# Attention's projection as two groups of seven block products, and the gate work that moves into the attention

## Chip, cores and metric

One core of a Trainium2 chip runs the kernel. The metric is the device time of one execution in microseconds, as the median of several runs; a profiled execution adds a trace of every engine: TensorE (PE, with its weight loads PEld), VectorE (DVE), ScalarE (ACT), GpSimd (POOL) and the queue engine SyncE (SP).

## What is computed

One layer of a transformer block over 512 tokens of width 2048, in fp32, with 256 context tokens. Cut to what matters here:

```
h   = rmsnorm(x) * (1 + scale) + shift                 # shift, scale, gate = silu(c) @ w_ada + b_ada
q, k, v, z_a, u_b, z_b, g_a, g_b = split(h @ w_in)     # 12 query heads, 4 key/value heads of 128
y_a = (attention(q, k, v) * silu(z_a)) @ w_proj_a      # 512 x 1536 times 1536 x 2048
y_b = (fourier_mix(u_b) * silu(z_b)) @ w_proj_b        # 512 x 512  times  512 x 2048
y   = (sigmoid(g_a) * y_a + sigmoid(g_b) * y_b) @ w_out
out = rmsnorm(x + gate * y) * final_g
```

## The kernel before

**Products.** Every fp32 operand is split into two fp32r parts, `hi` on ACT (line 163) and `lo = value - hi` on DVE (line 164), and a product is three matmuls (`mm3`, lines 311 to 313): hi x hi, hi x lo, lo x hi. A matmul is 128 x 128 against 128 x 512. Weights come in pieces of 128 x 1024 (512 KB); SP asks for them into a few raw slots (tiles `wr`), and each is split before PE uses it.

**Groups of seven block products.** The projections of `w_in` and `w_out` are done by a scheme of the Strassen kind (class `Group`, lines 756 to 852): rows, inner dimension and columns are halved, and seven products of blocks take the place of eight. `PRODUCTS` (line 55) names them P1, Q5, P2, Q6, P7, Q3, Q4. Some use sums of weight blocks. These are built in a chain: a tile `R` per piece (`chain`) holds the first block, is split for P1, then a DMA that adds (`accum_op`, issued by POOL, line 267) puts the next block on it, it is split for Q5, and so on for Q6 and Q4. `OUT_GROUP` (line 58) is the order P1, P2, Q5, Q6, P7, Q3, Q4. Results in PSUM are copied or subtracted out by ACT and DVE after a product.

**Attention** (lines 1135 to 1278). A loop of 48 steps (12 heads x 4 blocks of 128 queries): scores on PE, the maximum on DVE (line 1180), the exponential on ACT (line 1182), transposes on PE (line 1198), a split on ACT and DVE, and every second step the product with the values. What comes out is multiplied with the gate `z` (lines 1221 and 1222), kept per head in `branch`, and split into `S`. Between these steps PE gets 64 portions of the Fourier branch's projection (`filler`, line 1136): one bank of PSUM at a time, copied by ACT into `ybs` (line 1156).

**Attention's projection** (`products`, line 1229, and the loop at 1336). Four chunks of 512 columns in the order 0, 2, 1, 3. Each goes through six weight pieces (pairs of heads) with 24 matmuls a piece, over four banks of PSUM: 576 matmuls. The first chunk's first pieces run in the last steps of the attention. In this loop DVE also does three other things. It multiplies the Fourier chunks with their gate `gb` (line 1353). It works on the modulation's gate: 32 pieces `w_gate` of 128 x 1024 are multiplied with the condition row `crow` and summed along the row (`use_gate`, line 1038). And it multiplies each finished chunk with its gate `ga` and adds the Fourier part (lines 1372 and 1373). The merged chunk is transposed on PE (line 1299), and the sums and splits of token blocks that the output projection needs (`form`, line 1307) follow as `jobs`, one to a weight piece.

**Output projection.** Two groups of seven, 8 and 9, of four pieces a product.

**What sets the order.** Each engine works in order. A scheduler lays out the order within each engine at build time from the program's order and its own estimates; `issue_after` and `manual_schedule` pin some places. Slots for tiles are handed out by `take` and `give`, and a new user of a slot waits for the old one's last access. DMA queues are SP's (weights), ACT's (stores of projections) and POOL's (heads, gates, adding DMAs).

## Time and profile before

| what | us |
|---|---|
| median of 3 runs (1321.52 to 1322.96) | 1321.84 |
| span of the profiled execution, first to last instruction | 1320.2 |
| start to 822: all projections of `w_in`, the Fourier mix | 822 |
| attention, 822 to 1020 | 198 |
| attention's projection, 1020 to about 1155 | 135 |
| output projection and end, to 1320.2 | 165 |

The profiled execution's own time is taken as its span; the runs' median lies 1.6 us above it. The profile lists, for each engine, how long it was busy, what it waited for and who released it; a stretch of the span can be asked for by itself. Start times are microseconds from the span's first instruction.

### The profile page before, as it was taken

How to read it: one execution, taken by the hardware profiler on the slowest of the kernel's cores; microseconds unless marked ns; L12 is line 12 of the kernel's file. 1: busy time of each engine (PE TensorE's matmuls, PEld its weight loads, DVE VectorE, ACT ScalarE, POOL GpSimd, SP SyncE). 2: the span in 40 equal slices, each digit the busy share in tenths (PEclk: the TensorE clock that was granted, in tenths of full speed). 3: DMA queues.
4: the chain of work that ended last, by engine and by line, in shares of the span. 5: the costliest groups of instructions: out<-in, count | busy, mean ns of one | idle time of the engine just before them, and what ended most of it. 6: DMA issues, size and time to landing. Idle time of an engine off the chain costs nothing.

```text
span 1320.2 us, 17480 instructions
## 1 busy us (share of the span) xinstructions
PE 1296.7 (98%) x6594; PEld 1061.2 (80%) x6594; DVE 975.0 (74%) x1289; ACT 653.3 (49%) x1020; POOL 144.0 (11%) x192
## 2 busy tenths in 40 slices
PE   6999999999999999999999999999999999999997
PEld 3577887888888888888888887888888888888885
DVE  5666899878788868646487666677776789777676
ACT  5222655555555554444354454666666133355544
POOL 0110011110201111011031110000000100111210
PEclk9999999999999999999999999999999999999999
DMA  9898587887898998877669886122013889678985
GB/s 383 339 374 327 182 237 200 227 229 219 205 319 195 295 271 248 284 165 191 192 170 317 221 241 215 48 72 81 33 65 112 319 331 331 189 173 222 225 206 173
DMA packets 96228, 291.26 MB, mean 221 GB/s; under 512 B 8976, under 2 KB 32272, under 8 KB 91792
## 3 DMA queue, kind: packets, MB, share of 16 engines
q1 hardware_dynamic: 48720, 163.65, 35.4%
q0 software_dynamic: 22800, 96.49, 30.4%
q10 hardware_dynamic: 24624, 30.02, 6.6%
q8 instruction: 51, 0.84, 0.3%
q14 instruction: 33, 0.27, 0.1%
HBM read 263.37 MB, written 26.75 MB: 220 GB/s over the span
## 4 chain that ended last, share of the span: by engine, by line
PE 93%; DVE 3%; DMA 2%; issue 1%; ACT 1%; SPq 0%; DVEq 0%; ACTq 0%
PE banks L311 11%; PE banks L312 11%; PE banks L313 11%; PE x L312 8%; PE x L313 8%; PE x L311 8%; PE y L312 7%; PE y L313 7%; PE y L311 7%; PE banks L1198 3%; PE pd L493 2%; PE pb L311 2%; PE pb L313 1%; PE pb L312 1%; DMA wa<-in_w_ss 1%; PE pc L311 1%
## 5 line engine op out<-in xcount | busy, mean ns | idle before, releaser
L163 ACT ACTIVATE whi<-wr 128x1024 fp32r<-128x1024 f32 (+1 forms) x129 | 135.2, 1051 | 161.8 <-PE banks L313 91.5
L164 DVE TENSOR_TENSOR wlo<-wr,whi 128x1024 fp32r<-128x1024 f32 (+1 forms) x129 | 156.2, 1214 | 54.7 <-ACT whi L163 54.4
L164 DVE TENSOR_TENSOR wlo<-R,whi 128x1024 fp32r<-128x1024 f32 x114 | 138.8, 1222 | 68.5 <-ACT whi L163 68.5
L163 ACT ACTIVATE whi<-R 128x1024 fp32r<-128x1024 f32 x114 | 120.5, 1059 | 136.6 <-PE x L313 41.2
L311 PE MATMUL banks<-whi,s 128*128 128x512 f32 x420 | 165.9, 395 | 1.7 <-DVE ev L798 1.5
L312 PE MATMUL banks<-wlo,s 128*128 128x512 f32 x420 | 164.8, 392 | 0.0
L313 PE MATMUL banks<-whi,s 128*128 128x512 f32 x420 | 164.3, 391 | 0.0
L311 PE MATMUL x<-whi,s 128*128 128x512 f32 x352 | 137.3, 390 | 0.0
L313 PE MATMUL x<-whi,s 128*128 128x512 f32 x352 | 137.1, 389 | 0.0
L312 PE MATMUL x<-wlo,s 128*128 128x512 f32 x352 | 137.1, 389 | 0.0
L311 PE MATMUL y<-whi,s 128*128 128x512 f32 x316 | 123.2, 390 | 0.0
L312 PE MATMUL y<-wlo,s 128*128 128x512 f32 x316 | 123.0, 389 | 0.0
L313 PE MATMUL y<-whi,s 128*128 128x512 f32 x316 | 122.9, 389 | 0.0
L267 POOL DMA_DIRECT2D R<-in_w_g x64 | 55.4, 866 | 418.7 <-DVE wlo L164 234.6
L311 PEld LDWEIGHTS banks<-whi,s 128*128 128x128 f32 x420 | 78.9, 188 | 18.0 <-ACT whi L163 1.9
L163 ACT ACTIVATE s<-wr 128x512 fp32r<-128x512 f32 (+2 forms) x93 | 61.4, 678 | 63.4 <-PE y L312 16.3
L313 PEld LDWEIGHTS banks<-whi,s 128*128 128x128 f32 x420 | 78.9, 188 | 16.4
L312 PEld LDWEIGHTS banks<-wlo,s 128*128 128x128 f32 x420 | 79.0, 188 | 14.8
L164 DVE TENSOR_TENSOR s<-wr,s 128x512 fp32r<-128x512 f32 (+2 forms) x93 | 67.3, 751 | 21.4 <-ACT s L163 20.4
L313 PEld LDWEIGHTS x<-whi,s 128*128 128x128 f32 x352 | 66.1, 188 | 13.7
L311 PEld LDWEIGHTS x<-whi,s 128*128 128x128 f32 x352 | 66.1, 188 | 13.7
L312 PEld LDWEIGHTS x<-wlo,s 128*128 128x128 f32 x352 | 66.1, 188 | 13.6
(283 smaller groups left out, 2770.5 us busy)
## 6 DMA issues: line engine op xcount, KB each, us to landing
wr<-in_w_g SPq DMA_DIRECT2D x128, 512.0 KB, 4.9
R<-in_w_g POOLq DMA_DIRECT2D x64, 512.0 KB, 6.4
wa<-in_w_ss POOLq DMA_DIRECT2D x26, 1024.0 KB, 8.1
R<-in_w_g SPq DMA_DIRECT2D x32, 512.0 KB, 5.2
wr<-in_w_pab SPq DMA_DIRECT2D x32, 512.0 KB, 5.1
wr<-in_w_gate SPq DMA_DIRECT2D x32, 512.0 KB, 5.5
wr<-in_w_o SPq DMA_DIRECT2D x24, 512.0 KB, 6.6
R<-in_w_o POOLq DMA_DIRECT2D x24, 512.0 KB, 8.1
```

Of the source, the lines that this page charges most:

```text
L163: first = nc.scalar.activation(hi, src, ACT.Copy)
L164: return first, nc.vector.tensor_tensor(lo, src, hi.bitcast(F32), op=ALU.subtract)
L267: nc.gpsimd.dma_start(chain[e.pc], e.nxt, accum_op=ALU.add)
L311: nc.tensor.matmul(o, ah, bh, start=start, stop=False, skip_group_check=cont)
L312: nc.tensor.matmul(o, ah, bl, start=False, stop=False, skip_group_check=cont)
L313: nc.tensor.matmul(o, al, bh, start=False, stop=stop, skip_group_check=cont)
L493: last = nc.tensor.matmul(acc[32 * j : 32 * j + 32, :256], c2[:, 8 * h + k, :], w[:, k, :], start=n < 4, stop=n >= KK - 4)
L1198: nc.tensor.transpose(tp[:, k * P : (k + 1) * P], p[:, k * P : (k + 1) * P], ident)
```

## The change

Attention's result no longer goes through plain products. Its 1536 inner dimension is halved (heads 0 to 5 and 6 to 11), the tokens are halved (256 each) and the columns are two chunks each in two groups: group 10 has chunks 0 and 2, group 11 chunks 1 and 3. Each group is seven block products in `OUT_GROUP`'s order with three pieces a product. P7's weights are a raw block onto which a POOL DMA adds a second one (`onto`); Q4's are a fourth link of the chain. P1 of group 10 stands where the first chunk's first pieces stood, in the last steps of the attention.

```diff
-BRANCH_A, BRANCH_B = (0, 1, 2, 3, 4, 5), (6, 7)
+BRANCH_A, BRANCH_B = 10, (6, 7)
+A_CHUNKS = ((0, 2), (1, 3))
...
             e.raws.append((p, raw))
+            if e.onto is not None:
+                nc.gpsimd.dma_start(raw, e.onto, accum_op=ALU.add)
...
-    def stream_product(name, g, w, by_dve):
+    def stream_product(name, g, w, by_dve, pieces=4):
...
-            if isinstance(what, tuple):
+            if isinstance(what, tuple) and name == "P7" and g >= BRANCH_A:
+                stream(key, [part(1)], 1024, 2, pc=pc, onto=part(2))
+            elif isinstance(what, tuple):
...
-                       nxt=part(what + 1) if what < 2 and what + 1 not in by_dve else None)
+                       nxt=part(what + 1) if what < (3 if g >= BRANCH_A else 2) and what + 1 not in by_dve else None)
...
-    for n, j in enumerate(CHUNKS):
-        for pc in BRANCH_A:
-            stream(("pab", j, pc), w_pab[j, pc], 1024, 2)
+    for n in range(2):
+        for name in OUT_GROUP:
+            stream_product(name, BRANCH_A + n, BranchWeights(n), (), 3)
```

The Fourier branch gets its gate inside the attention: DVE multiplies each portion out of PSUM with the gate, which POOL's DMA has loaded into one of the chain's tiles or a slot, in place of ACT's copy, and the result goes to memory (`yb_d`).

```diff
-                nc.scalar.copy(y[:, t % 2, :], acc)
+                nc.vector.tensor_tensor(y[:, t % 2, :], acc, y[:, t % 2, :], op=ALU.mult)
+                if t % 2:
+                    nc.gpsimd.dma_start(yb_d[t // 2, j], flat(y))
```

Attention's output is kept per pair of heads (`AT`), its token halves are split as blocks A11, A12 and A22, and four forms of sums and differences are made for each of three pairs of pairs, two of them in the loop and one at its end.

```diff
+    def branch_forms(q):
+        u, v = AT[q], AT[q + 3]
+        lo, hi = slice(0, 256), slice(256, 512)
+        branch_form("S3", q, u[:, :, lo])
+        nc.vector.tensor_tensor(u[:, :, hi], u[:, :, hi], v[:, :, hi], op=ALU.subtract)
+        branch_form("Z5", q, u[:, :, hi])
...
```

The modulation's gate leaves DVE and the old projection loop. In steps 2 to 38 of the attention POOL multiplies the two halves of each row of weights with the condition row and adds them, 48 units in all, and ACT sums along the row. Both condition rows are now loaded and put through silu at the start of the attention. The 32 loads of `w_gate` move with them.

```diff
+    def gate_unit(u):
+        kb, part = divmod(u, 3)
+        if part < 2:
+            w = gw[part] = get_aside(("gate", kb + KK * part))
+            if kb + 1 < KK:
+                ask_gate(kb + 1 + KK * part)
+            nc.gpsimd.tensor_tensor(w, w, crow[part], op=ALU.mult)
+        else:
+            w = gw[0]
+            nc.gpsimd.tensor_tensor(w, w, gw[1], op=ALU.add)
+            nc.scalar.activation(w, w, ACT.Copy, scale=0.5, accum_out=gparts[:, kb : kb + 1])
...
+        if i >= 2:
+            for u in range(4 * (i - 2) // 3, min(4 * (i - 1) // 3, 3 * KK)):
+                gate_unit(u)
```

A finished chunk half is multiplied with its gate, a POOL DMA adds the Fourier part from `yb_d` to it, and five pieces later in the program it is transposed. The forms for the output projection are tied to counts of pieces (`after`, `form_at`).

```diff
+    def branch_done(n, half, c, v, t):
+        j = A_CHUNKS[n][c]
+        t = take((2, 512)) if t is None else t
+        w = ga.pop((half, j))
+        nc.vector.tensor_tensor(t, v, w, op=ALU.mult)
+        give(w)
+        nc.gpsimd.dma_start(flat(t), yb_d[half, j], accum_op=ALU.add)
+        merged[j, half] = t
+        after(5, lambda: turn_merged(j, half))
```

Smaller edits: weights of `V` are split only when they are due; the heads' loads come one step later; the old loop with `products`, `use_gate` and its gate loads is gone.

More of the change, by code (lines that the diff above doesn't have):

```diff
@@ L726, in pair @@
     def pair(tag, skip=0):
+        if isinstance(tag, int):
+            return banks[0][:, tag : tag + 2, :] if tag < 6 else banks[1]
         if banks:
@@ L769, in run, with steps @@
         def run(self, name):
+            for _ in self.steps(name):
+                pass
+        def steps(self, name):
             form, which = next((f, c) for n, f, _, c in PRODUCTS if n == name)
```

281 lines of the change are left out of this document (160 added, 121 removed).

## Prediction

> **What bounds the kernel now.** First the page's head, then the chain that ended last, then the windows of the stages that the change touches. The columns of a window row: its length, busy us and count of PE, PEld, DVE, ACT, POOL, then the granted clock, the DMA share and GB/s.
>
> ```profile
> span 1320.2 us, 17480 instructions
> PE 1296.7 (98%) x6594; PEld 1061.2 (80%) x6594; DVE 975.0 (74%) x1289; ACT 653.3 (49%) x1020; POOL 144.0 (11%) x192
> ...
> PE 93%; DVE 3%; DMA 2%; issue 1%; ACT 1%; SPq 0%; DVEq 0%; ACTq 0%
> ```
> ```profile
> 822.00:1020.00 198.00, 196.65 (x1305) 171.74 (x1303) 145.42 (x251) 125.12 (x221) 4.58 (x9) 1.00 0.21 71
> 1020.00:1060.00 40.00, 40.00 (x189) 33.52 (x187) 28.96 (x35) 9.25 (x10) 5.96 (x12) 1.00 0.83 305
> 1060.00:1100.00 40.00, 40.00 (x191) 33.38 (x190) 35.50 (x45) 12.22 (x15) 1.06 (x2) 1.00 0.90 334
> 1100.00:1150.00 50.00, 50.00 (x234) 41.69 (x233) 40.91 (x49) 19.31 (x23) 3.68 (x5) 1.00 0.80 261
> 1150.00:1235.00 85.00, 84.77 (x379) 69.63 (x379) 64.00 (x55) 43.90 (x52) 15.01 (x18) 1.00 0.82 196
> ```
>
> TensorE bounds every stage: it never stops in the projection (1020 to 1150) and stands still for 1.35 of 198 us in the attention, at full clock. So a matmul taken out is worth its whole cadence, and a stall put in costs its whole length: there is no slack on PE to pay for it. Beside it the attention uses the DMA engines at 0.21 and POOL for 4.6 us, and the projection uses the DMA engines at 0.80 to 0.90.
>
> **What it removes.** The old projection is 4 chunks x 6 weight pieces x 24 matmuls = 576 of 128x512. The new one is 2 groups x 7 products x 3 pieces x 12 = 504; transposes (64), score, value and Fourier matmuls stay. So 72 go. Their cadence stands in the timeline of the old projection:
>
> ```profile
> 1039.93 0.39 PE L313 MATMUL banks<-whi,s 128*128 128x512 f32 x1
> ...
> 1045.82 0.39 PE L312 MATMUL banks<-wlo,s 128*128 128x512 f32 x1
> ```
>
> Between these two starts lie 26 matmuls: 5.89 / 26 = 0.2265 us each. 72 x 0.2265 = **16.3 us less**, if nothing new stalls PE.
>
> **What it moves into the attention: the gate sums.** 32 products on DVE (1.22 us each, hidden in the old projection) become 32 products and 16 sums on POOL, with 16 passes on ACT that add up along the row. Operations of this kind POOL does nowhere in the old trace, so I bound one:
>
> ```profile
> L443 POOL MEMSET s<- 128x512 f32 x1 | 0.5, 529 | 0.0
> L1627 POOL MEMSET const-bfloat16-1.0<- 128x1 bf16 x1 | 0.1, 106 | 0.0
> L871 POOL TENSOR_SCALAR small<-small 128x8 f32<-128x8 f32 (+2 forms) x11 | 5.9, 534 | 100.7 <-ACT cxe L968 63.4 <-DVE small L986 18.4 <-ACT y L883 17.7
> L1050 POOL DMA_DIRECT2D s<-qz_d x12 | 6.4, 534 | 169.8 <-PE banks L313 47.4 <-DVE s L164 37.5 <-issue 28.0
> ```
>
> A fill costs (529 - 106) / 511 = 0.83 ns per element, one stream. 1024 elements at one stream: 0.11 + 0.85 = **0.95 us**, the low end. Arithmetic on 8 elements costs 0.53; with two reads and a write one after another, 0.53 + 3 x 0.85 = **3.1 us**, the high end. I take 0.53 + 2 x 0.85 = **2.2 us**, nearest to the arithmetic row, with the two reads in turn and the write beside them. A page gives a price: by the Trainium skill, "GPSIMD Engine Reference", section 3 "Performance versus the Vector engine", an fp32 tensor_tensor of 2048 elements takes 4497 ns on GpSimd, so about 2.3 us for 1024 (an estimate from that page), by which the sum below would be some 2 us higher; no run here shows it yet.
>
> 48 x 2.2 = 106 us of POOL would hide in 198. But the engines run in order, and in the built order ACT's passes stand between the exponentials: pass 1 ahead of exponential 1, pass 2 ahead of exponential 2, 3 ahead of 4, 4 ahead of 5, 5 ahead of 7, 6 ahead of 8, 8 ahead of 12, 10 ahead of 17. Behind a pass wait the exponential, then its transposes on PE, and PE has nothing else in its order. And the gate's weight loads wait for slots that the gate before gives back: SP loads one part of pair k+1 when POOL's sum k is done, the other when a pass is done. The rows for this ladder, by the old clock:
>
> ```profile
> 807.89 1.23 DVE L798 TENSOR_TENSOR ev<-y,ev 128x1024 f32<-128x1024 f32 x1 [2.26 <-PE y L313]
> ...
> L1031 DVE SCALAR_TENSOR_TENSOR s<-s,s 128x1024 f32<-128x1024 f32 x1 | 1.2, 1224 | 0.0
> ```
> ```profile
> L1030 ACT ACTIVATE s<-s 128x1024 f32<-128x1024 f32 x1 | 1.1, 1053 | 0.0
> L1182 ACT ACTIVATION_READ_ACCUMULATOR s<-banks,gain 128x1 f32 x48 | 9.4, 196 | 0.0
> wr<-in_w_gate SPq DMA_DIRECT2D x1, 512.0 KB, 3.7
> ```
> ```profile
> 814.51 1.06 ACT L163 ACTIVATE whi<-wr 128x1024 fp32r<-128x1024 f32 x1 [1.23 <-PE x L313]
> 825.09 0.90 ACT L1182 ACTIVATE s<-banks,gain 128x768 f32<-128x768 f32 x1 [1.06 <-DVE gain L1180]
> 827.51 0.90 ACT L1182 ACTIVATE s<-banks,gain 128x768 f32<-128x768 f32 x1 [0.95 <-DVE gain L1180]
> 865.46 0.90 ACT L1182 ACTIVATE s<-banks,gain 128x768 f32<-128x768 f32 x1 [0.39 <-DVE gain L1180]
> ```
>
> The condition row is ready behind that eviction and one 1.22 us product: 807.89 + 1.23 + 1.22 = 810.3. Sum 1: three POOL operations and one DMA issue, 810.3 + 6.6 + 0.53 = 817.4; its pass (1.05 + 0.20 = 1.25) ends at 818.7. Sum 2: a load (3.7 and 0.3 for its issue = 4.0), four POOL operations (one belongs to pair 3) and an issue: 818.7 + 4.0 + 8.8 + 0.53 = 832.0. Exponential 2 stands behind its pass: 833.3 in place of 827.5, 5.8 late. Sums 3 to 5 have one part loaded early: 4.0 + 2 x 2.2 = 8.4 each, 857.2. Sums 6 to 8 wait for both parts: 4.0 + 3 x 2.2 = 10.6 each, 889.0. Pass 8 and a weight split (1.06) then stand ahead of exponential 12: 891.3 in place of 865.5, **26 us late**. Pass 10 is no later, and after exponential 17 no pass stands until exponential 24, so POOL gets ahead. PE cannot make up lost time: the attention grows by 26 us. With 0.95 us the same ladder gives, behind the split that ends at 815.6, 816.8 for pass 1 and 825.1 for sum 2, which then waits for exponential 1; steps of 5.9, then of 7.4 (the pass and a load now limit); exponential 12 is 2 to 4 late: **3**. With 3.1 us: 838.3, steps of 10.2 and 13.3, 908.8: **46**.
>
> **The rest of what moves there.** DVE gets 16 products in place of ACT's 16 copies, 8 splits and 8 sums of the forms and a few more: some 36 operations of 0.69 us, 25 us on top of 145.4 of 198; ACT loses 16 copies (0.585) and gets 16 passes and 8 splits, 17 us more on 125.1. Both fit beside PE; if that cover fails, it fails by the order above, already counted. I cost them at nothing.
>
> **The branch groups.** Weights now go through a chain in SBUF to which a DMA adds the next block. Prices from the old output projection, where such adds run (its 75 us from 1160 to 1235; the row "to landing" is that of the chain's transfers between 1150 and 1260):
>
> ```profile
> DMA packets 4166, 15.22 MB, mean 203 GB/s; under 512 B 460, under 2 KB 460, under 8 KB 4162
> ## 3 DMA queue, kind: packets, MB, share of 16 engines
> q0 software_dynamic: 2002, 7.30, 54.0%
> q1 hardware_dynamic: 2160, 7.87, 30.3%
> ```
> ```profile
> DMA to landing us min/median/max: 3.9/7.6/16.3
> 1240.00:1250.00 10.00, 10.00 (x46) 8.20 (x45) 5.58 (x5) 5.96 (x8) 4.53 (x6) 1.00 1.05 213
> L1198 PE MATMUL banks<-ident,s 128*128 128x128 f32 x288 | 43.3, 277 | 0.1
> ```
>
> q0 carries the adds: 0.540 x 75 / 7.30 = 5.55 us per MB, 2.9 us for one of 0.524 MB. A plain load: 0.303 x 75 / 7.87 = 2.89 us per MB, 1.5 us. From the attention's end to the last product of group 2 the built order has about 26 adds (17 on the chain, 4 on a raw tile, 5 or 6 of the merged chunks) and 34 plain transfers, the first loads of the output projection among them: 26 x 2.9 + 34 x 1.5 = 126 us. PE needs 468 x 0.2265 + 48 transposes x 0.15 = 113 us. If the DMA engines work at the 1.05 that a 10 us window reached, 126 / 1.05 = 120 us: **8 us of stall** (rounded up from 7, for the third block product, due 8.2 us after the second with a median add of 7.6, and the first turned chunk, due 8.2 us after a 1.2 us product and that add). Bounds: 0 (attention's free DMA takes more of it early; the old output projection ran at 0.82 with 0.23 us of PE idle) and 18 (126 - 113 and two late adds).
>
> **Sum**, against the profiled execution's own 1320.2: -16.3 + 26 + 8 = +17.7, 1337.9. The median of the runs shown, 1321.84, lies 1.6 above that span: **1339.5 us**.
>
> **Rivals.** *A, faster:* POOL's operation near a fill's 0.95 us. For it: 0.83 ns per element; against it: 0.53 us for 8 elements of arithmetic. -16.3 + 3 + 8 = -5: 1316.5, and 1308 without the DMA stall. It decides at the price where the ladder costs 8.3: (8.3 - 3) / (26 - 3) of the way from 0.95 to 2.2, 1.24 us. *B, dearer POOL:* 3.1 us, because POOL and DVE hold each other up at SBUF. -16.3 + 46 + 8: 1359. Against it: in the attention DVE's operations with both inputs in SBUF are few:
>
> ```profile
> L164 DVE TENSOR_TENSOR wlo<-wr,whi 128x1024 fp32r<-128x1024 f32 x9 | 11.0, 1224 | 1.8 <-ACT whi L163 1.8
> L164 DVE TENSOR_TENSOR s<-s,s 128x512 fp32r<-128x512 f32 x11 | 7.5, 686 | 2.1 <-ACT s L163 2.1
> ```
>
> That is 18.5 of 198 us. By the Trainium skill, "GPSIMD Engine Reference", section 1 "Specifications", GpSimd shares its SBUF interfaces with VectorE and contends with instructions of DVE that have two SBUF inputs; by these rows it would find few to contend with. *C, the DMA engines bind:* 18 in place of 8, the gates as forecast: 1349.5. *D, the change does what it says and nothing else:* passes and adds all hidden, 1305.5; for it only that POOL and DMA engines are free in the sum.
>
> **How the numbers follow.** Forecast 0.48, A 0.18, B 0.10, C 0.17, D 0.07. The range 1313 to 1354 takes in the forecast, C and most of A, and leaves out D and B. A measurement of this kernel tells about 0.2% (2.6 us) from no change. Faster: D and most of A, 0.23; within: the edge of A and short gates with long DMA stalls, 0.06; slower 0.71.
>
> **What would show it.** PE instructions down by 72. POOL's product of 128x1024 at 2.2 us. In the first 70 us of the attention ACT idle ahead of the passes, released by POOL's sums; PE idle there by some 26 us, next to none in the second half. In the branch groups PE idle on splits or turned chunks whose adds land late, some 8 us, with the DMA share near 1. It is wrong if POOL's operation takes under 1.24 us, if the passes never wait, or if the branch groups stall PE by over 18 us.

## The result, and the profile after

The changed kernel takes 1391.55 us (median of 4 runs, 1384.27 to 1393.09), the kernel before 1321.8 beside it: 1.0514 times as long, 95% interval 1.0489 to 1.054. The profiled execution took 1390.56 us with a span of 1388.8, which is 68.6 more than before. The forecast was 1339.5 with a range of 1313 to 1354: slower, as forecast, but by 70 us in place of 18.

The head of the page, and the shares of the chain that ended last:

```profile
span 1388.8 us, 17575 instructions
...
PE 1302.5 (94%) x6522; PEld 1062.5 (77%) x6522; DVE 1014.4 (73%) x1277; ACT 689.6 (50%) x1063; POOL 292.2 (21%) x280
```
```profile
PE 75%; DMA 8%; POOL 6%; DVE 5%; issue 3%; ACT 2%; POOLq 0%; SPq 0%; DVEq 0%; ACTq 0%
```

TensorE has 72 instructions less, as the sum had it, and yet it now holds only 75% of the chain, where it held 93%. The stages show where it stands (busy us and count of PE, PEld, DVE, ACT, POOL, granted clock, DMA share, GB/s):

```profile
822.00:1020.00 198.00, 150.89 (x893) 129.41 (x894) 148.30 (x191) 96.71 (x174) 118.39 (x62) 0.91 0.49 164
1020.00:1084.00 64.00, 62.95 (x409) 55.18 (x410) 54.62 (x95) 41.83 (x73) 7.76 (x12) 0.97 0.48 115
1084.00:1124.00 40.00, 36.36 (x176) 30.32 (x175) 24.82 (x30) 19.03 (x23) 9.53 (x13) 1.00 0.98 251
1124.00:1164.00 40.00, 32.14 (x149) 26.17 (x148) 23.75 (x20) 16.51 (x16) 7.12 (x9) 0.97 0.88 230
```

In the 198 us in which the attention ran from end to end before, TensorE is now busy for 150.89 (it was 196.65). GpSimd is busy for 118.39 of them. After 1020, when the last gate is done, TensorE is full again; in the branch groups it stops a second time (32.14 of 40 us).

A ruler for the rest is the start of the exponentials on ScalarE, from the timelines of both kernels:

| exponential | 1 | 12 | 17 | 24 | 34 | 48 | end of span |
|---|---|---|---|---|---|---|---|
| before, us | 825.1 | 865.5 | 886.6 | 917.9 | 956.2 | 1012.5 | 1320.2 |
| after, us | 831.2 | 900.9 | 924.3 | 960.4 | 1018.9 | 1076.7 | 1388.8 |
| later by | 6.1 | 35.4 | 37.7 | 42.5 | 62.7 | 64.2 | 68.6 |

So of the 68.6 us, 6.1 are lost ahead of the first exponential, 58.2 between exponentials 1 and 48 and 4.3 from there to the end (differences of the unrounded starts). The last number is 16.3 us of matmuls saved and 20.6 us newly lost: behind exponential 48 TensorE stands idle for 26.0 us in place of 9.3, and its granted clock there is 0.97 in place of 0.99.

Three views of the attention. First the waits from 815 to 1085 (total us, times, longest):

```profile
POOL wr L1329 <- DMA wr<-in_w_gate: 47.1, 16, 6.7
ACT wr L1333 <- POOL wr L1332: 43.9, 13, 5.3
```

The gate's ladder is there as forecast: GpSimd waits for gate weights, ScalarE stands at the passes. GpSimd's operations in the same window (mean ns behind the busy us):

```profile
L1332 POOL TENSOR_TENSOR wr<-wr,wr 128x1024 f32<-128x1024 f32 x16 | 39.7, 2482 | 1.0
L1329 POOL TENSOR_TENSOR wr<-wr,crow 128x1024 f32<-128x1024 f32 x16 | 39.1, 2445 | 15.6 <-DMA wr<-in_w_gate 14.3 <-ACT R L1276 0.7 <-ACT s L1235 0.6
```

2.45 to 2.48 us each, a little above the 2.2 taken. And the one group of VectorE that changed most, the 128x128 division of each exponential's step, from 830 to 1020, before and after:

```profile
L1192 DVE TENSOR_SCALAR s<-s,gain 128x128 f32<-128x128 f32 x46 | 13.0, 286 | 1.4
```
```profile
L1245 DVE TENSOR_SCALAR s<-s,gain 128x128 f32<-128x128 f32 x33 | 37.9, 1150 | 0.9
```

The same operation on the same data takes four times as long in the mean. The mean is made of two kinds: from 815 to 1085 the median is still 0.29 us, 14 of 47 divisions take over 1 us, and the longest takes 3.61. One example from VectorE's timeline and, below it, GpSimd's:

```profile
852.50 2.35 DVE L1245 TENSOR_SCALAR s<-s,gain 128x128 f32<-128x128 f32 x1
```
```profile
852.31 2.46 POOL L1332 TENSOR_TENSOR wr<-wr,wr 128x1024 f32<-128x1024 f32 x1
```

It starts while a GpSimd operation runs and ends with it, at 854.8. Two others outlast the operation in which they begin: the one of 3.61 us at 833.82 and one of 3.30 us at 988.87 end with a second GpSimd operation that follows the first at once. VectorE's operations that read PSUM keep their lengths (the maximum: 950 ns before and after). By the Trainium skill, "SBUF — State Buffer", "Who interferes with whom", a `tensor_scalar` can enter a two-port mode in which it needs the pair of ports that GpSimd uses, and whoever comes second waits for the whole instruction of the other. This row agrees, the two longer ones go beyond it, and the runs below test it.

### The profile page after: what moved, and what is told of

Its sections match the earlier page's. It is cut to its first block, busy times and chain, and to the rows that moved or that the text cites. A ratio compares the mean times of both kernels' runs of the same rounds, so it can differ in the third digit from the quotient of the medians.

```text
span 1388.8 us, 17575 instructions
## 1 busy us (share of the span) xinstructions
PE 1302.5 (94%) x6522; PEld 1062.5 (77%) x6522; DVE 1014.4 (73%) x1277; ACT 689.6 (50%) x1063; POOL 292.2 (21%) x280
## 4 chain that ended last, share of the span: by engine, by line
PE 75%; DMA 8%; POOL 6%; DVE 5%; issue 3%; ACT 2%; POOLq 0%; SPq 0%; DVEq 0%; ACTq 0%
PE x L319 8%; PE x L320 8%; PE x L318 8%; PE y L319 7%; PE y L320 7%; PE y L318 7%; PE banks L318 6%; PE banks L320 6%; PE banks L319 6%; POOL wr L1329 3%; DMA wr<-in_w_gate 3%; DMA s<-yb_d 3%; POOL wr L1332 2%; PE pd L510 2%; DMA wr<-in_w_pab 2%
## 5 line engine op out<-in xcount | busy, mean ns | idle before, releaser
L167 DVE TENSOR_TENSOR wlo<-R,whi 128x1024 fp32r<-128x1024 f32 x138 | 167.9, 1221 | 90.2 <-ACT whi L166 89.6
L166 ACT ACTIVATE whi<-R 128x1024 fp32r<-128x1024 f32 x138 | 145.9, 1059 | 170.4 <-PE banks L320 46.8
L167 DVE TENSOR_TENSOR wlo<-wr,whi 128x1024 fp32r<-128x1024 f32 (+1 forms) x123 | 150.7, 1229 | 60.9 <-ACT whi L166 60.9
L166 ACT ACTIVATE whi<-wr 128x1024 fp32r<-128x1024 f32 (+1 forms) x123 | 128.4, 1049 | 101.3 <-PE y L320 36.7
L318 PE MATMUL banks<-whi,s 128*128 128x512 f32 x396 | 158.9, 401 | 9.9 <-DVE ev L833 4.9
L319 PE MATMUL banks<-wlo,s 128*128 128x512 f32 x396 | 156.9, 396 | 0.9 <-DVE wlo L167 0.9
L320 PE MATMUL banks<-whi,s 128*128 128x512 f32 x396 | 156.9, 396 | 0.0
L318 PEld LDWEIGHTS banks<-whi,s 128*128 128x128 f32 x396 | 75.6, 191 | 26.3 <-issue 5.3
L166 ACT ACTIVATE s<-wr 128x512 fp32r<-128x512 f32 (+2 forms) x93 | 61.7, 678 | 67.4 <-PE y L319 16.3
L319 PEld LDWEIGHTS banks<-wlo,s 128*128 128x128 f32 x396 | 75.6, 191 | 15.6 <-DVE wlo L167 1.3
L320 PEld LDWEIGHTS banks<-whi,s 128*128 128x128 f32 x396 | 75.4, 190 | 15.6
```

What stands on the lines that cost most here:

```text
L166: first = nc.scalar.activation(hi, src, ACT.Copy)
L167: return first, nc.vector.tensor_tensor(lo, src, hi.bitcast(F32), op=ALU.subtract)
L318: nc.tensor.matmul(o, ah, bh, start=start, stop=False, skip_group_check=cont)
L319: nc.tensor.matmul(o, ah, bl, start=False, stop=False, skip_group_check=cont)
L320: nc.tensor.matmul(o, al, bh, start=False, stop=stop, skip_group_check=cont)
```

## The experiments

The first theory was the prediction's ladder, now for all 16 gates: the load in the loop, GpSimd's operations, and the pass in front of an exponential. Its rivals were VectorE's added work, contention in SBUF and the clock. The table gives all runs: the median, and from the profiled execution of each the time between exponentials 1 and 48 and from there to the end.

| kernel | us | ratio to before (95%) | exp. 1 to 48 | 48 to end |
|---|---|---|---|---|
| before | 1321.8 | 1 | 187.4 | 307.8 |
| changed | 1391.55 | 1.0514 (1.0489 to 1.054) | 245.5 | 312.1 |
| no gates | 1342.63 | 1.0158 (1.0143 to 1.0173) | 187.0 | 318.0 |
| no gate loads | 1392.21 | 1.0528 (1.0512 to 1.0544) | 238.1 | 315.1 |
| own slot, pass later | 1382.17 | 1.0456 (1.0438 to 1.0474) | 232.1 | 315.2 |
| products on VectorE | 1352.42 | 1.0227 (1.0205 to 1.0249) | 206.6 | 315.7 |
| passes tied | 1384.31 | 1.0471 (1.0455 to 1.0486) | 242.1 | 310.3 |
| GpSimd alone | 1383.84 | 1.0476 (1.0444 to 1.0509) | 234.1 | 311.7 |
| GpSimd alone, halves | 1371.19 | 1.0371 (1.0351 to 1.039) | 221.6 | 314.0 |
| GpSimd alone, division on ScalarE | 1354.72 | 1.025 (1.0235 to 1.0266) | 198.7 | 315.8 |
| changed, division on ScalarE | 1397.61 | 1.0561 (1.054 to 1.0581) | 254.6 | 316.8 |
| tied, division on ScalarE | 1377.87 | 1.0422 (1.0406 to 1.0439) | 239.6 | 309.5 |
| the same, gate loads by GpSimd | 1387.64 | 1.0492 (1.0471 to 1.0513) | 240.8 | 317.6 |
| the same, no gate loads | 1358.65 | 1.028 (1.0255 to 1.0305) | 209.1 | 315.3 |
| Fourier part early | 1381.87 | 1.0447 (1.043 to 1.0464) | 246.7 | 304.8 |
| no Fourier part | 1376.21 | 1.0413 (1.0397 to 1.0428) | 246.3 | 298.2 |
| tied, early, raw pieces | 1377.85 | 1.0422 (1.0406 to 1.0437) | 244.0 | 303.6 |
| tied, division, early | 1371.31 | 1.0377 (1.0358 to 1.0395) | 238.0 | 303.9 |
| VectorE gates, division, early, raw pieces | 1341.75 | 1.0159 (1.0141 to 1.0177) | 208.4 | 302.5 |
| no gates, early | 1327.53 | 1.0048 (1.0031 to 1.0064) | 186.9 | 317.6 |

### Is it the gates, and what in them?

**No gates.**

```diff
     def gate_unit(u):
...
-        kb, part = divmod(u, 3)
...
+        pass
...
-    for q in (0, KK):
-        ask_gate(q)
+    nc.vector.memset(gparts, 0.0)
```

> The changed kernel without its 16 gate sums: no gate weights are loaded, GpSimd makes no products and sums of them, ScalarE no passes, and the gate column is the bias alone (this part of the computation is left out). Theory (the gates' ladder of load, three GpSimd operations and ScalarE's pass in front of an exponential paces the attention from the first gate to the last): exponential 1 to 48 comes back from 245.5 us to about 187, as before the change; 1391.5 - 58 - up to 6 = 1327 us (1320 to 1337), under 5 us above the kernel before. Rival 'the Fourier gate and the forms of the branch load VectorE and delay the attention by themselves': the 58 us stay for the most part, 1375 or more. Rival 'clock': the granted clock stays near 0.98 and the time at 1370 or more.

Measured: 1342.63 us. Between exponentials 1 and 48 it takes 187.0 us, the 187.4 of before. So the Fourier gate and the forms of the branch, some 25 us more on VectorE, cost the attention nothing, as the prediction had it, and the whole 58 us are the gates'. The rival of the clock is out with that. Of the 15.6 us above the 1327 expected, 5.9 lie behind exponential 48 (318.0 us in place of 312.1) and are not explained; the rest lies ahead of the first exponential and comes from the edit itself: with no gates the gate column is ready at once, and its store (2048 single numbers) goes out at 3.1 us, in the middle of the kernel's first loads. First the changed kernel, then this one:

```profile
0.00:50.00 50.00, 39.87 (x235) 22.38 (x236) 25.52 (x54) 22.63 (x39) 5.31 (x17) 1.00 0.95 379
```
```profile
0.00:50.00 50.00, 33.30 (x173) 17.01 (x174) 17.60 (x40) 19.02 (x34) 5.41 (x16) 1.00 0.96 315
```

62 matmuls fewer in the first 50 us; the first exponential comes at 834.9. The three kernels with GpSimd alone share this, although their edit ties the gate column to the last exponential: their store goes out at 3.1 us too. So they are compared with this one.

**No gate loads.** GpSimd's operations and the passes stay at their places, on resident data.

```diff
-            w = gw[part] = get_aside(("gate", kb + KK * part))
-            if kb + 1 < KK:
-                ask_gate(kb + 1 + KK * part)
-            nc.gpsimd.tensor_tensor(w, w, crow[part], op=ALU.mult)
...
+            nc.gpsimd.tensor_tensor(gt[part], crow[0], crow[1], op=ALU.mult)
```

> The changed kernel with all of GpSimd's 48 operations and ScalarE's 16 passes at their places, but on data that stay in SBUF: no gate weight is loaded (the gate comes out otherwise; heads 10 and 11 are loaded one step later, for two slots more). Theory (it is the load in the loop, 4 us of some 11.5 a gate, that makes the ladder slower than the 9 us that two and a quarter steps of the attention take): 3 x 2.46 + 1.06 = 8.4 us and hand-overs a gate against 9, so nearly all of the 64 us comes back: 1327 to 1345 us, the first gates still pushing exponentials by a few us each. Rival 'GpSimd's operations slow VectorE's and ScalarE's by sharing SBUF': 1370 to 1390, with the mean of VectorE's operations in the attention longer than in the kernel without gates. Rival 'any pass that waits for GpSimd in ScalarE's queue costs its whole ladder': 1360 to 1380.

Measured: 1392.21 us, no gain. The loads that the ladder waited for are gone, and what waits instead is ScalarE, more than before:

```profile
ACT s L1332 <- POOL s L1331: 62.4, 16, 6.9
```

The passes come 7 to 10 us apart, GpSimd's own pace, all 16 before exponential 15. The place of the passes in ScalarE's queue is fixed when the kernel is built, and it is too early here as well; it is not the same place, since pass 13 now stands ahead of exponential 12, where the changed kernel has pass 8. So the load is not needed for a loss of this size, and the first theory falls as it was put. What share the passes have in this run, and what share VectorE's waits for GpSimd, it cannot say.

**Own slot, pass later in the program.**

```diff
+            if part == 0:
+                gw[0] = take((1024,))
+            nc.gpsimd.tensor_tensor(gw[part], w, crow[part], op=ALU.mult)
...
+            while len(gsum) > (1 if i < 33 else 0):
+                gate_pass()
```

> The changed kernel with the ladder taken apart and all of its work kept: GpSimd's first product goes to a slot of its own, so its weight tile goes back to the loads after one operation in place of after ScalarE's pass; the sum lies in that slot and ScalarE's pass of it stands one gate later in ScalarE's queue (heads 10 and 11 are loaded one step later, for slots). Theory: loads hide behind GpSimd's 7.4 us a gate, below the attention's 9, and no exponential waits for a sum: 1325 to 1345 us. Rival 'GpSimd's and DMA's traffic in SBUF slows the other engines': stays at 1375 or more although no pass waits. Rival 'the order of SP's queue (gate loads behind loads that wait for slots) keeps them late': 1350 to 1375, GpSimd waiting for gate weights.

Measured: 1382.17 us. The edit did not do what it was for: when the kernel was built the passes moved forward again, 14 of 16 waited for their sums, 47.3 us in all. It tells nothing on the port.

**Passes tied.** The same, with each pass tied behind an exponential.

```diff
-        nc.scalar.activation(w, w, ACT.Copy, scale=0.5, accum_out=gparts[:, kb : kb + 1])
+        with tc.issue_after(exps[-1].ins):
+            nc.scalar.activation(w, w, ACT.Copy, scale=0.5, accum_out=gparts[:, kb : kb + 1])
```

> As the kernel with its own slot for the sum, but each of ScalarE's 16 passes is tied behind an exponential whose program place is at least two steps after its sum (first pass behind exponential 10), so that its place in ScalarE's queue no longer follows the order found when the kernel is built. All work is kept. Theory as it now stands (the loss in the attention is ScalarE standing in its in-order queue at passes whose sums GpSimd has not made yet: 62 us of waits without any load, 47 us with the own slot; the load in the loop is not needed for it): exponential 1 to 48 back to 187 to 197 us, 1330 to 1346 us, waits of ScalarE for GpSimd under 10 us. Rival 'GpSimd and the added loads slow the attention by themselves': 1365 or more with no such waits. Rival 'GpSimd then falls behind its own queue (loads and stores that wait)': the passes wait again, 1350 to 1375.

Measured: 1384.31 us. Now no pass waits for GpSimd, and the attention still takes 242.1 us between exponentials 1 and 48. The division's row from 830 to 1020, and a wait that was not there before:

```profile
L1245 DVE TENSOR_SCALAR s<-s,gain 128x128 f32<-128x128 f32 x36 | 31.6, 879 | 1.0
```
```profile
ACT whi L166 <- DMA wr<-in_w_pab: 17.3, 2, 10.9
```

The passes are therefore not the only holder. Two others are in sight: VectorE's division, three times its length, and splits of the Fourier product's weights that come late.

**Products on VectorE**, in the attention, each with its row sum; no GpSimd arithmetic, no passes.

```diff
-            nc.gpsimd.tensor_tensor(w, w, crow[part], op=ALU.mult)
...
+            with tc.issue_after(last_split[-1][1].ins):
+                nc.vector.scalar_tensor_tensor(w, w, 0.5, crow[part], op0=ALU.mult, op1=ALU.mult,
+                                               accum_out=gparts[:, q : q + 1])
```

> The changed kernel with the gates' products made by VectorE in the attention (one operation with its sum for each of the 32 weight tiles, as the kernel before made them later; no GpSimd operations, no ScalarE passes), loads at the same places. Theory: no exponential waits for GpSimd any more, but 32 x about 1.2 = 39 us more on VectorE, busy 0.75 of 187 us before and some 25 us more by the forms: 1.1 of the time, so VectorE binds: 1345 to 1360 us. Rival 'VectorE's added work is the cause of the loss now': slower than the changed kernel or the same, 1385 to 1410. Rival 'the place of the gates in the attention costs nothing once GpSimd is out': 1325 to 1335.

Measured: 1352.42 us, in the range of the theory. The same products, as 39 us of work on VectorE, are 39 us faster than on GpSimd.

### GpSimd by itself

**GpSimd alone.** No loads, no passes; 48 operations whose results nobody reads, paced by the exponentials' row sums.

```diff
+        k = (len(exps) - 1) % 4
+        e = stats[:, 4 * k + 1 : 4 * k + 2].broadcast_to([P, 1024])
+        a, b = ((crow[0], e), (crow[1], e), (gt[0], gt[1]))[part]
+        nc.gpsimd.tensor_tensor(gt[part % 2], a, b, op=ALU.mult if part < 2 else ALU.add)
```

> No gate weights are loaded and ScalarE makes no passes (the gate column is the bias alone, stored at the end of the attention); GpSimd makes 48 operations of 128x1024 whose results nobody reads, each paced by an exponential's row sum. So of the gates only GpSimd's own work is left. New theory, 'port': VectorE's operations with all operands in SBUF (in every exponential's step the 128x128 division, 0.29 us alone, 1.15 mean in the changed kernel) stand still until GpSimd's operation in progress ends; VectorE is busy 0.80 of the attention without gates, so 30 to 40 us of such waits make it the bound: exponential 1 to 48 in 200 to 222 us against 187 without the gates, 1344 to 1366 us, the division's mean over 0.7 us. Rival 'queues alone' (ScalarE's passes and SP's loads in their in-order queues made the whole loss): 187 to 191 us, 1330 to 1337, although GpSimd is busy.

Measured: 1383.84 us, 41.2 more than without gates, and 234.1 in place of 187.0 us between exponentials 1 and 48: above the expected range, and far from the rival's 1337. The division, from 815 to 1085:

```profile
L1245 DVE TENSOR_SCALAR s<-s,gain 128x128 f32<-128x128 f32 x48 | 52.9, 1106 | 1.2
```

and in the kernel without gates:

```profile
L1245 DVE TENSOR_SCALAR s<-s,gain 128x128 f32<-128x128 f32 x48 | 13.5, 286 | 1.1
```

Nobody waits for the results of these operations, and they cost 41 us. Besides VectorE's wait, the DMAs that stand behind them in GpSimd's queue could do that; the run with the division on ScalarE, below, keeps that queue and bounds what it can cost.

**In halves.** Each operation cut into two of 128x512.

```diff
-        nc.gpsimd.tensor_tensor(gt[part % 2], a, b, op=ALU.mult if part < 2 else ALU.add)
+        for c in (slice(0, 512), slice(512, 1024)):
+            nc.gpsimd.tensor_tensor(gt[part % 2][:, c], a[:, c], b[:, c], op=ALU.mult if part < 2 else ALU.add)
```

> As the kernel with GpSimd's 48 operations alone, but each cut into two of 128x512 (96, by the element's share 1.2 to 1.5 us each). Port theory with the wait lasting to the end of the one operation in progress: the longest wait of a 128x128 division falls from some 2.4 to 1.3 us and their mean to 0.5 to 0.8, 1336 to 1355 us and 5 to 15 us below the kernel with whole operations. Rival 'the two engines share a bandwidth': the division's mean and the time as with whole operations, or longer by the added fixed costs.

Measured: 1371.19 us, 12.7 less than with whole operations, though the time itself is above the range. VectorE's division and GpSimd's operations beside it:

```profile
852.49 0.87 DVE L1245 TENSOR_SCALAR s<-s,gain 128x128 f32<-128x128 f32 x1
...
854.33 1.03 DVE L1245 TENSOR_SCALAR s<-s,gain 128x128 f32<-128x128 f32 x1
```
```profile
851.06 2.22 POOL L1331 TENSOR_TENSOR s<-crow,gain 128x512 f32<-128x512 f32 x2 [0.40 <-ACT s L1235]
853.24 2.04 POOL L1331 TENSOR_TENSOR s<-s,gain 128x512 f32<-128x512 f32 x2
855.24 2.52 POOL L1331 TENSOR_TENSOR s<-s,s 128x512 f32<-128x512 f32 x2
```

The two divisions end at 853.4 and 855.4, each with the half operation in which it began (a row holds two of them); the median division falls from 860 to 629 ns. GpSimd does the same elements and more fixed cost, so a shared bandwidth would have made it no better. The length of one GpSimd instruction matters. It does not bound the wait, however: the longest division was expected at 1.3 us and takes 6.98, over six half operations behind a DMA issue:

```profile
901.97 6.98 DVE L1245 TENSOR_SCALAR s<-s,gain 128x128 f32<-128x128 f32 x1
```
```profile
901.84 0.55 POOL L1202 DMA_DIRECT2D yb_d<-R  x1
902.41 2.05 POOL L1331 TENSOR_TENSOR s<-crow,gain 128x512 f32<-128x512 f32 x2
904.41 2.02 POOL L1331 TENSOR_TENSOR s<-s,gain 128x512 f32<-128x512 f32 x2
906.40 2.47 POOL L1331 TENSOR_TENSOR s<-s,s 128x512 f32<-128x512 f32 x2
```

Why VectorE gets no turn between them here, and does at 853.4, is open.

**Division on ScalarE**, with GpSimd alone.

```diff
-        nc.vector.tensor_scalar(z, z, r, None, op0=ALU.mult)
+        nc.scalar.mul(z, z, r)
```

> As the kernel with GpSimd's 48 operations alone, but the 128x128 division is made by ScalarE. Port theory: VectorE's operations of the attention that are left read PSUM for the most part and do not wait for GpSimd; only the splits and sums with both inputs in SBUF do (some 20 in the attention): exponential 1 to 48 in 187 to 198 us, 10 us or more below the kernel with the division on VectorE, 1331 to 1345 us. Rival 'any VectorE operation pays when GpSimd works': no lower than that kernel. Rival 'ScalarE cannot take 48 more operations': ScalarE's queue delays the exponentials, the same or later, without long VectorE operations.

Measured: 1354.72 us, 29 less than with the division on VectorE. Exponentials 1 to 48 take 198.7 us (expected 187 to 198): one operation of 0.29 us carried three quarters of the 47 us, and all else that GpSimd's operations do, its queue included, costs 12 us at most. A part of the gain may be the division's own 13.5 us of work, which VectorE is rid of as well; the kernel without gates was not run with the division on ScalarE. The time lies 10 above the range; this family starts its exponentials late (837.3 in place of 825.1).

### What holds the changed kernel itself

**The division moved, all else as changed.** The same edit as the last, on the changed kernel.

> The changed kernel with one edit: the 128x128 division of every exponential's step is made by ScalarE. Gate loads, GpSimd's operations and ScalarE's passes stay as they are. It divides the loss between the port and the ladder of the prediction (load, three GpSimd operations, pass in front of an exponential). Port theory (VectorE's waits for GpSimd are what binds): 20 to 35 us less, 1356 to 1372 us. Ladder theory (gates 11.4 us apart by 4.0 + 3 x 2.46, whatever VectorE does): 1382 to 1394, with ScalarE's waits for GpSimd longer than 44 us in the attention, since VectorE no longer comes late.

Measured: 1397.61 us, 6 more than the changed kernel. That is 4 above the range of the ladder theory, but its sign is there:

```profile
ACT wr L1333 <- POOL wr L1332: 55.4, 15, 6.5
```

With VectorE free of the wait, ScalarE only stands longer at the passes (43.9 before). So in the changed kernel the gates' pace binds for the most part, and the port is a second cause that would bind if the first were gone. It does show in places: between 968.7 and 982.7 the chain that ended last goes through three stretched VectorE operations (two divisions and a difference of token halves, 0.29 and 0.69 us in the run without gates):

```profile
968.68 2.27 DVE s L1245
...
976.97 3.39 DVE s L1287
...
980.47 2.17 DVE s L1245
```

**Both taken away**: "passes tied" with the division on ScalarE, the two edits shown.

> The kernel with tied passes (1384.3 us) with the division on ScalarE as well: neither the passes nor the division wait for GpSimd. Theory (both causes, each enough to hold the attention near its slow pace): 1345 to 1362 us, exponential 1 to 48 in 200 to 215, what is left being weight loads behind gate loads in SP's queue and the splits with both inputs in SBUF. Rival 'port and ladder were not it': 1375 or more.

Measured: 1377.87 us, the rival's side: a third holder. The chain around the longest hole (exponential 31 at 969.0, 32 at 988.6) is in four rows, of GpSimd, of SP and of ScalarE:

```profile
978.10 2.34 POOL L1335 TENSOR_TENSOR s<-s,wr 128x1024 f32<-128x1024 f32 x1
```
```profile
958.71 19.67 SPq L203 DMA_DIRECT2D wr<-in_w_gate  x5
980.46 0.33 SPq L203 DMA_DIRECT2D wr<-in_w_pab  x1
```
```profile
986.41 1.06 ACT L166 ACTIVATE whi<-wr 128x1024 fp32r<-128x1024 f32 x1 [15.50 <-DMA wr<-in_w_pab]
```

GpSimd's sum ends at 980.44; SP's load of weights for the Fourier product, behind five gate loads, goes out at 980.46; ScalarE's split of them, in the queue ahead of exponential 32, waits 15.5 us. Four such waits make 27.3 us.

**Gate loads from GpSimd's queue**, and **no gate loads**, both on that kernel.

```diff
-            asks[0].dma_start(raw if len(src.shape) == 2 else raw.rearrange("p (i j c) -> p i j c", i=4, j=2), src)
+            (nc.gpsimd if e.aside else asks[0]).dma_start(raw if len(src.shape) == 2 else raw.rearrange("p (i j c) -> p i j c", i=4, j=2), src)
```

> The kernel with tied passes and the division on ScalarE (1377.9 us, exponential 1 to 48 in 239.5), with one edit: gate weights are loaded from GpSimd's queue in place of SP's. Theory (a third cause that takes the place of the other two: weights of the Fourier products stand in SP's in-order queue behind gate loads that wait for slots; ScalarE's weight splits wait 27.3 us for them, three holes in the row of exponentials of 13 to 20 us): the holes go, 33 us less in the attention, 1340 to 1356 us. Rival 'the holes are DMA traffic, not order': 1370 or more. Rival 'loads issued by GpSimd wait in turn behind its operations': gates late, 1355 to 1370.

> The kernel with tied passes and the division on ScalarE, with no gate weights loaded (GpSimd's products on the condition row, so the gate comes out otherwise; operations and passes at the same places). Theory: neither ladder, nor division, nor loads in SP's queue; what is left of the gates are VectorE's splits and sums with both inputs in SBUF, as in the kernel with GpSimd alone and the division on ScalarE (198.8 us): exponential 1 to 48 in 195 to 208, 1333 to 1350 us. Rival 'the tied passes on ScalarE cost by themselves': over 215 us, 1355 or more.

Measured: 1387.64 us with the loads in GpSimd's queue; the same wait is still there, 32.0 us in four times. So it is not that they stand behind gate loads in SP's queue. The rows of the longest of the four, of SP and of ScalarE:

```profile
985.86 17.07 SPq L203 DMA_DIRECT2D wr<-in_w_pab  x3
```
```profile
989.56 1.06 ACT L166 ACTIVATE whi<-wr 128x1024 fp32r<-128x1024 f32 x1 [18.94 <-DMA wr<-in_w_pab]
```

The time is that of the rival "DMA traffic, not order", but the first of these loads lands within 3.7 us of going out: it came late because it went out late. With no gate loads it is 1358.65 us, 209.1 between exponentials 1 and 48: the attention is 1 above its range, and the time 9 above its own, on the side of the rival of the tied passes, whose 215 us of attention it does not reach. So the gate loads do hold the attention, for 30 of the 239.6 us. That they do it through the shared raw slots, which a gate weight keeps until GpSimd has read it, fits the rows above (the load goes out as the sum ends), but is argued: a kernel with more slots was not tried.

### The branch groups

**Fourier part early**: loaded beside its gate and added by VectorE; and **left out**.

```diff
-        nc.gpsimd.dma_start(flat(t), yb_d[half, j], accum_op=ALU.add)
+        nc.vector.tensor_tensor(t, t, y, op=ALU.add)
```

> The changed kernel with the gated Fourier part of each output chunk loaded into a slot beside its gate, ahead of time, and added by VectorE, in place of the adding DMA that starts only when the chunk is multiplied. The attention is as in the changed kernel. Theory (the turned chunks wait for late adding DMAs, 27 us of waits at the transposes, some 17 us of TensorE idle in the branch groups): 8 to 15 us less, 1376 to 1384 us. Rival 'DMA traffic binds this stage, whichever way the bytes come': 1388 to 1394. Rival 'VectorE's 8 further additions of 1.2 us come out on the path': 1390 to 1400.

> The changed kernel without the addition of the Fourier part (8 adding DMAs of 512 KB left out, the output lacks that part). Theory: the bound of what those DMAs cost, 10 to 17 us less than the changed kernel: 1374 to 1382. Rival 'the stage is bound by its weight loads (34 plain, 26 adding)': 1386 to 1392.

Measured: 1381.87 and 1376.21 us, 9.7 and 15.3 less than the changed kernel, both as the theory had it. TensorE's longest wait from exponential 48 on in the changed kernel was the first row; with the part early it is the second:

```profile
PE banks L1359 <- DMA s<-yb_d: 14.1, 5, 8.0
```
```profile
PE banks L318 <- ACT s L841: 8.0, 2, 4.2
```

From exponential 48 to the end it is 312.1 us in the changed kernel, 298.2 without the part; 307.8 - 16.3 = 291.5 would be no stall at all. So 13.9 of the 20.6 us go with these eight adding DMAs, and 6.7 are the rest.

### Versions

The first is "passes tied" with the early Fourier part and with two raw pieces for the seventh product, the second is "tied, division on ScalarE" with the early part, the third "products on VectorE" with the division on ScalarE, the early part and the raw pieces:

```diff
-                stream(key, [part(1)], 1024, 2, pc=pc, onto=part(2))
+                stream(key, [part(1), part(2)], 1024, 2, pc=pc)
```

> Passes tied behind exponentials, sum in its own slot, Fourier part loaded early and added by VectorE, and for the seventh product the two weight parts loaded side by side and added by VectorE in place of an adding DMA on GpSimd's queue. All work is kept. Theory: 1391.5 - 50 (attention) - 8 to 20 (branch groups): 1318 to 1333 us, beside the kernel before. Rival 'DMA binds the branch groups': 1335 to 1343. Rival 'the attention stays slow': 1360 or more.

> As the kernel before it in this list, with the Fourier part loaded early and added by VectorE. Theory: 7 to 10 us less than that one, 1337 to 1353 us, still slower than the kernel before the change. Rival 'it was the adding DMAs' place only while the attention was slow': no more than 3 us less.

> All work of the changed kernel, GpSimd without arithmetic: gate products on VectorE in the attention (1352.4 us with that alone), the 128x128 division on ScalarE (13.7 us less on VectorE, which was at 1.01 of the time by its sums and comes to 0.94), the Fourier part loaded early and added by VectorE (9.6 less when done alone), two weight tiles side by side for the seventh product. Theory: 1352.4 - 13 - 8 = 1331 us (1320 to 1340). Rival 'VectorE's order, not its sum, paces the attention': 1338 to 1346. Rival 'DMA binds the branch groups': no gain there, 1337 to 1341.

Measured: 1377.85, 1371.31 and 1341.75 us. The first fell short because tying the passes did, the second by what the kernel under it had missed; the early Fourier part is worth 6.6 us in it, a little under what was expected. The third, with all work kept, is the fastest form found: GpSimd without arithmetic, the part loaded early. It is still 1.6% slower than before the change. Its branch groups gain 13.2 us (302.5 in place of 315.7). Its attention takes 208.4 us, no less than with the gates on VectorE alone, so taking the division off VectorE did not help there: the rival "VectorE's order, not its sum" is nearer.

**No gates, Fourier part early**, with the gate column formed after the last exponential.

```diff
+    nc.vector.tensor_scalar(gparts[:, :KK], stats[:, :KK], 0.0, None, op0=ALU.mult)
     nc.vector.tensor_tensor(gcol, gparts[:, :KK], bada[:, 2 * KK :], op=ALU.add)
```

> No gates at all (no loads, products, passes; the gate column is the bias alone, formed after the last exponential, so that its store of single numbers does not lie in the first loads of the kernel), Fourier part loaded early and added by VectorE. It is the floor of the other two thirds of the change: the groups of seven products and the Fourier gate in the attention. Theory: attention as before the change (187 us), branch groups 16.3 us less for TensorE and some 10 of it lost to late weights and chunks: 1391.5 - 58 - 10 = 1323 us (1314 to 1331). Rival 'the groups of seven cost as much as they save': 1327 to 1335.

Measured: 1327.53 us, inside the ranges of both theory and rival, so it does not decide between them; it is 0.5% above the kernel before, and not clean either. The store of the gate column now goes out at 1024.5, in the first loads of the branch groups. Two windows of that stage:

```profile
1030.00:1035.00 5.00, 4.60 (x20) 3.83 (x21) 3.76 (x7) 3.38 (x6) 0.00 (x0) 1.00 0.53 28
...
1050.00:1055.00 5.00, 0.00 (x0) 0.00 (x0) 0.00 (x0) 0.00 (x0) 0.00 (x0) 0.66 1.07 271
```

The DMA engines are half busy at 28 GB/s, and 15 us later TensorE stands still for want of late weights; in 1020 to 1060 it lacks 13.3 us. That all of this comes from the store is argued. If it does, the two other parts of the change alone would come to some 1318 us (an estimate for the profiled execution, 1331.6 - 13.3; it was the slowest of five), hardly below the kernel before; no run shows it.

## Why the prediction was wrong

- **Matmuls, -16.3 us:** right in the count (6594 to 6522).
- **GpSimd's operation, 2.2 us taken:** 2.45 to 2.48, inside the bounds. The price in the Trainium skill, "GPSIMD Engine Reference", section 3, gave some 2.3 (an estimate from that page); the trace agrees within 10%. Rival A is out by this.
- **Ladder of the first half, +26 us:** the mechanism was right, the size short. Exponential 12 is 35.4 us late, 6.1 of it already at exponential 1. Pass 1 ends 3 us later than worked out, and from gate 5 on passes come some 11 to 12 us apart where 10.6 was worked out; 4.2 for the load as measured and three times 2.46 make 11.6.
- **The step that failed: "Pass 10 is no later, and after exponential 17 no pass stands until exponential 24, so POOL gets ahead."** GpSimd did not get ahead in that gap. Its queue holds more than products:

```profile
930.29 2.39 POOL L1329 TENSOR_TENSOR wr<-wr,crow 128x1024 f32<-128x1024 f32 x1 [0.57 <-ACT s L1235]
950.36 0.58 POOL L1085 DMA_DIRECT2D s<-qz_d  x1 [17.69 <-issue]
```

It stood for 17.7 us ahead of a head's load, for no reason that the profile names. What made pass 11 late is in the chain that ended last:

```profile
946.98 0.12 PE banks L1097
947.12 0.33 SPq L203
947.54 4.47 DMA wr<-in_w_gate
952.24 4.71 POOL wr L1329 x2
956.95 2.34 POOL wr L1332
```

SP sent the next gate loads at 947.1, right behind the last transpose of raw keys (line 1097 of the changed kernel); that the keys' slot is what they waited for is the profile's reading, and no run tests it. The sum ended at 959.3, and pass 11 came then, 36 us behind pass 10, after 5 us of waiting in front of exponential 24. From exponential 17 to 34 the attention lost 25 us more, where the prediction had nothing: TensorE stood idle for 28.0 us from 822 to 925, and for another 19.1 from there to 1020, the stretch that was to have next to none. Waits at passes 11 to 16 are 11.4 us of these (13 and 15 waited for nothing); the chain goes through gate loads, late weights of the Fourier product and stretched VectorE operations as well, and their shares are not separated. The price of a ladder that goes on to the last unit is not that of its first half.
- **VectorE's and ScalarE's added work, nothing:** right for the work itself (187.0 us without gates). But it was the wrong question. VectorE lost by waiting.
- **Rival B** had the cause in the wrong place. It priced the contention on GpSimd's operation (3.1 us) and was put aside because VectorE's operations with two SBUF inputs are few, 18.5 of 198 us. The section of the Trainium skill cited there ("GPSIMD Engine Reference", section 1) names a second kind too, instructions in a two-port mode, which the prediction passed over. The division has one SBUF input, runs in all 48 steps, and pays (a mean of 0.29 without gates, 0.89 in the changed kernel). The few with two SBUF inputs paid too: splits of 128x256 took 1.15 us in place of 0.42. Alone, GpSimd's arithmetic costs 41 us, three quarters of it by the division. In the changed kernel that lies behind the ladder for the most part, as the run with only the division moved shows.
- **Branch groups, +8 us:** 20.6 lost, beyond its own bound of 18; as added idle time of TensorE alone it is 16.7. Work was priced as a sum of DMA time against TensorE's; 13.9 of it are the eight additions to turned chunks, which can start only when a chunk is done; loading them ahead gave back 7.3 (304.8 us from exponential 48 on).

What was left out as a whole is that three holders stood side by side: the passes, VectorE's wait and the gate loads. VectorE's wait alone is enough to hold the attention near its slow pace (234.1 us with GpSimd alone), and so are the gate loads with the other two taken away (239.6); passes alone were not run. So undoing one changed the time by between 7 us less (passes tied) and 6 more (division), two by 14 less; all three by 33 less, 36 of the 58 between the exponentials (245.5 to 209.1). The other 22 are still lost beside GpSimd's operations, and their cause stays open.

## What to carry to other kernels

Arithmetic on GpSimd is not free because GpSimd is idle: count first the VectorE operations that keep all their operands in SBUF and stand in each step of the loop, and give each a wait (here 0.6 to 0.8 us in the mean for a division, beside operations of 2 to 2.5 us, and several of them at the worst). Do not end a ladder's price where its first gap lies; take its pace per unit against the loop's and carry it to the last unit. When undoing one suspect brings nothing, undo two at a time before dropping it, and see whether work by itself, with no one waiting for it, already costs the time.

## What the runs showed of the hardware that was not expected

- A 128x128 division with one input in SBUF takes 0.29 us, and beside GpSimd's arithmetic often the rest of a 2.46 us operation more; at the worst it took 3.61 us in the changed kernel, 4.28 with GpSimd alone, and 6.98 with GpSimd's operations in halves. Operations of VectorE that read PSUM keep their time (950 ns for 128x768).
- A GpSimd sum or product of 128x1024 takes 2.39 to 2.56 us with two full inputs and 1.95 us when one is a single number per row (the kernel with GpSimd alone).
- The store of 2048 single numbers holds the DMA engines for some 10 us: 28 GB/s at half their time. Inside the attention it is hidden (at 1018.8 in the changed kernel, TensorE then busy for 62.95 of 64 us); in the first 50 us TensorE lacks 6.6 us with it (33.30 against 39.87 without), and 13.3 us at the start of the branch groups, where its share is argued.
- Where TensorE stands, its granted clock falls: 0.91 over 822 to 1020 in the changed kernel, 1.00 before; 0.66 in the 5 us in which it stood still in the run without gates, Fourier part early.
